# The beginning of a one-core encoder layer: order of the first loads, splits and products changed

## The chip, the cores and the metric

The kernel runs on one core of a Trainium2 chip. The metric is the device time of one launch in microseconds, the median over several runs, lower is better. One further execution is recorded by the hardware profiler; it has a time of its own and a span, which is the time from its first instruction to its last.

## What is computed

One residual layer over 512 tokens of width 1024. All matrix products are of float32 quality.

```python
h = rmsnorm(x, norm_w)                       # x: 512 x 1024
proj = h @ w_in + b_in                       # 11272 columns: q, k, v, gates of two mixers, merge gates
y_m = mlstm(...)                             # 4 heads of 256, chunkwise, conv + SiLU on q and k
y_s = stick_breaking_attention(...)          # 8 heads of 128, rmsnorm on q and k
merged = g_m * (y_m @ w_proj_m) + g_s * (y_s @ w_proj_s)
x = x + merged @ w_out
```

Only the beginning matters here: the rmsnorm of `x`, its transposition, and the first group of 512 columns of `proj` (the first four heads' `q` of the attention).

## The kernel before

**Products in three parts.** Each operand `a` is split into a high part (a rounded copy in the format that TensorE multiplies at full rate) and a low part, `a` minus the high part. A product is three TensorE products: high by high, low by high, high by low. The high part is a copy on ACT or DVE, the low part a subtraction on DVE or POOL.

**Units.** The weights come in units of 512 KB (`Unit`). A unit has a load (`load`, one DMA from the SP queue, line 109), a split (`split`, `wh` on ACT and `wl` on DVE, lines 90 and 91) and products (`mm(0)`, `mm(1)`). The main loop `for c in range(N)` goes through the units in order, splitting some units ahead, and weaves the other work between `mm(0)` and `mm(1)`. All orders are written by hand (the pools run under a manual schedule): an engine executes its instructions in the order in which the program gives them, and an instruction that waits holds up all behind it on that engine.

**The tokens.** `x` lies in four blocks of 128 tokens, `x_t[0]` to `x_t[3]`. `x_scale(tb)` makes the sum of squares of a block on ACT (lines 271 and 274, with a read of the accumulator behind each), the factor on POOL (lines 260 and 261) and multiplies the block on DVE (line 276). `x_turn(tb)` transposes the scaled block on TensorE in two groups of four tiles (line 286) and takes each group out of PSUM as high part `hh` (line 288, one DVE instruction for four tiles) and low part `hl` (line 292, four DVE instructions).

**The first four units are special.** They hold the same 512 columns for eight tiles of the depth, `k` = 0 to 7, two to a unit, and `units[tb]` stands for the products of token block `tb` with all eight (`first_mm(tb)`): 24 products. Their high parts are named `fh` (line 890, ACT), their low parts `fl` (line 891, DVE for the units 0 and 2, POOL for 1 and 3). For each `k` the three products stand side by side: `fh` by `hh` (line 932), `fh` by `hl` (line 933), `fl` by `hh` (line 934).

**What surrounds them.** `warm(n)` issues n products on a tile of zeros (`idle`, line 910). Before the main loop the program gives: nine such products, the transposition of `norm_w` (line 217), `x_scale(0)`, two more, `first_split(0)`, `x_turn(0)`, `first_split(1)` with POOL, `x_scale(1)`, `first_split(2)`, `first_split(3)` with POOL. In the loop, `x_turn(c + 1)` stands between the two halves of units 0 and 1, `x_scale(2)` and `x_scale(3)` stand behind the first of them, and `x_turn(3)` behind the second half of unit 1. The fourth unit's load goes to a tile of another pool (`P5`, shown as `P`).

## Time and profile before

| | |
|---|---|
| median of 3 runs | 719.27 us (718.88 to 719.35) |
| the profiled execution, its own time | 720.13 us |
| its span | 718.4 us |
| TensorE products (PE) busy | 709.8 us, 99% of the span |
| VectorE (DVE) busy | 424.5 us, 59% |
| ScalarE (ACT) busy | 315.8 us, 44% |
| GpSimd (POOL) busy | 93.5 us, 13% |
| mean granted TensorE clock | 0.997 of full |

A step that starts TensorE's dense work earlier or later by a microsecond moves the end by as much, as long as nothing behind it has to wait. All times of instructions are in microseconds from the start of the span.

### The profile page before, as it was taken

What the parts mean: (1) busy time and instruction counts of PE and PEld (TensorE: products, weight loads), DVE (VectorE), ACT (ScalarE), POOL (GpSimd) and SP (SyncE); (2) the same over time, 40 slices, a digit from 0 to 9 for tenths busy, and PEclk for the clock granted to TensorE, in tenths of its full rate; (3) what the DMA queues carried; (4) which work ended last, traced back from release to release, by engine and by line L of the source; (5) the groups of instructions that cost most, each with busy time, mean ns of one, the idle gap of its engine ahead of it and who ended that gap; (6) DMA issues with size and microseconds to landing.
All of it is one profiled execution on the core that took longest, in us unless ns stands there. A gap on an engine that the chain in (4) does not pass through costs nothing.

```text
span 718.4 us, 9058 instructions
## 1 busy us (share of the span) xinstructions
PE 709.8 (99%) x3356; PEld 593.1 (83%) x3356; DVE 424.5 (59%) x663; ACT 315.8 (44%) x601; POOL 93.5 (13%) x235
## 2 busy tenths in 40 slices
PE   7999999999999999999999999999999999999997
PEld 5888888888888888888888888888888888888886
DVE  5837886656487568279944737994343254556441
ACT  5245364476255544244475534447554343222210
POOL 5422022253022112000001110000112000000000
PEclk9999999999999999999999999999999999999999
DMA  6433332233323222333332233333223333333621
GB/s 239 133 103 81 109 86 77 69 95 92 99 62 87 58 86 62 102 91 97 101 94 59 63 99 88 91 100 89 74 59 89 89 91 97 104 88 89 234 89 58
DMA packets 91475, 67.80 MB, mean 94 GB/s; under 512 B 3470, under 2 KB 77608, under 8 KB 91432
## 3 DMA queue, kind: packets, MB, share of 16 engines
q1 hardware_dynamic: 91432, 67.23, 32.8%
q8 instruction: 26, 0.43, 0.2%
q14 instruction: 17, 0.14, 0.1%
HBM read 65.12 MB, written 2.10 MB: 94 GB/s over the span
## 4 chain that ended last, share of the span: by engine, by line
PE 97%; DMA 1%; DVE 1%; POOL 0%; SPq 0%; issue 0%; ACT 0%; DVEq 0%
PE dps L85 28%; PE dps L87 27%; PE dps L86 27%; PE aps L86 2%; PE aps L87 2%; PE aps L85 2%; PE aps L440 1%; PE aps L382 1%; DMA stg<-in_w_in_dram 1%; PE dps L934 1%; PE dps L932 1%; PE dps L933 1%; PE aps L735 1%; PE aps L736 1%; PE aps L737 1%; DVE fl L891 0%
## 5 line engine op out<-in xcount | busy, mean ns | idle before, releaser
L91 DVE TENSOR_TENSOR wl<-stg,wh 128x1024 fp32r<-128x1024 f32 x108 | 132.3, 1225 | 140.3 <-ACT wh L90 139.9
L85 PE MATMUL dps<-hh,wh 128*128 128x512 f32 x448 | 175.8, 392 | 0.0
L86 PE MATMUL dps<-hl,wh 128*128 128x512 f32 x448 | 174.6, 390 | 0.0
L87 PE MATMUL dps<-hh,wl 128*128 128x512 f32 x448 | 174.6, 390 | 0.0
L90 ACT ACTIVATE wh<-stg 128x1024 fp32r<-128x1024 f32 x108 | 113.6, 1052 | 95.3 <-PE dps L87 58.6
L87 PEld LDWEIGHTS dps<-hh,wl 128*128 128x128 f32 x448 | 84.1, 188 | 17.7
L85 PEld LDWEIGHTS dps<-hh,wh 128*128 128x128 f32 x448 | 84.2, 188 | 17.5 <-issue 1.0
L86 PEld LDWEIGHTS dps<-hl,wh 128*128 128x128 f32 x448 | 84.2, 188 | 16.6
L85 PE MATMUL dps<-wh,hh 128*128 128x512 f32 x224 | 88.3, 394 | 0.0
L87 PE MATMUL dps<-wh,hl 128*128 128x512 f32 x224 | 87.4, 390 | 0.0
L86 PE MATMUL dps<-wl,hh 128*128 128x512 f32 x224 | 87.4, 390 | 0.0
L87 PEld LDWEIGHTS dps<-wh,hl 128*128 128x128 f32 x224 | 42.1, 188 | 8.9
L86 PEld LDWEIGHTS dps<-wl,hh 128*128 128x128 f32 x224 | 42.1, 188 | 8.2
L85 PEld LDWEIGHTS dps<-wh,hh 128*128 128x128 f32 x224 | 42.1, 188 | 8.2
L626 DVE SCALAR_TENSOR_TENSOR acc<-tmp,vec,acc 128x511 f32<-128x511 f32 (+2 forms) x48 | 36.0, 750 | 1.7
L629 ACT ACTIVATE tmp<-acc 128x512 f32<-128x512 f32 x16 | 10.1, 633 | 50.2 <-DVE acc L626 50.2
L415 DVE TENSOR_TENSOR_SCAN om<-om 128x512 f32<-128x512 f32 (+3 forms) x32 | 27.9, 871 | 6.3 <-POOL om L409 6.3
L409 POOL TENSOR_SCALAR_AFFINE_SELECT om<-om 128x128 f32<-128x128 f32 x32 | 12.1, 378 | 134.5 <-ACT om L407 134.5
L90 ACT ACTIVATE at_split<-aps 128x384 fp32r<-128x384 f32 (+1 forms) x24 | 11.8, 525 | 36.8 <-PE aps L440 36.8
L688 POOL TENSOR_SCALAR_AFFINE_SELECT w_all<-om 128x128 f32<-128x128 f32 x16 | 4.1, 293 | 168.9 <-DVE om L683 168.9
L91 DVE TENSOR_TENSOR at_split<-aps,at_split 128x384 fp32r<-128x384 f32 (+1 forms) x24 | 13.7, 599 | 19.8 <-ACT at_split L90 19.8
L86 PE MATMUL dps<-wl,mgh 128*128 128x512 f32 x64 | 24.9, 389 | 0.0
(239 smaller groups left out, 1170.6 us busy)
## 6 DMA issues: line engine op xcount, KB each, us to landing
stg<-in_w_in_dram SPq DMA_DIRECT2D x87, 512.0 KB, 3.7
stg<-in_w_proj_s_dram SPq DMA_DIRECT2D x8, 512.0 KB, 3.7
stg<-in_w_proj_m_dram SPq DMA_DIRECT2D x8, 512.0 KB, 3.6
stg<-in_w_out_dram SPq DMA_DIRECT2D x8, 512.0 KB, 3.7
brow<-in_b_in_dram SPq DMA_DIRECT2D x8, 256.0 KB, 4.2
xr<-in_x_dram SPq DMA_DIRECT2D x8, 256.0 KB, 5.7
out_dram<-xr SPq DMA_DIRECT2D x7, 256.0 KB, 2.3
x<-in_x_dram SPq DMA_DIRECT2D x3, 512.0 KB
```

What stands on the lines that cost most here:

```text
L85: nc.tensor.matmul(ps, ah, bh, start=first, stop=False)
L86: nc.tensor.matmul(ps, ah, bl, start=False, stop=False)
L87: nc.tensor.matmul(ps, al, bh, start=False, stop=last)
L90: nc.scalar.activation(hi, src, AF.Copy)
L91: nc.vector.tensor_tensor(lo, src, hi.bitcast(F32), op=OP.subtract)
L382: nc.tensor.transpose(tp[:, tb * 128:(tb + 1) * 128], self.raw[name][tb][:, hs], ident)
L409: nc.gpsimd.affine_select(out=om[:, ts], in_=om[:, ts], compare_op=OP.is_gt, fill=1.0, base=0, channel_multiplier=1, pattern=[[-1, 128]])
L415: nc.vector.tensor_tensor_scan(back, back, back, 1.0, op0=OP.mult, op1=OP.bypass)
L440: nc.tensor.transpose(tp[:, at + (i - j) * 128:at + (i - j + 1) * 128], a_t[i][:, j * 128:(j + 1) * 128], ident)
L626: nc.vector.scalar_tensor_tensor(acc[:, j:], t[:, 0:T - j], cw(3 - j, ch), acc[:, j:], op0=OP.mult, op1=OP.add)
L629: nc.scalar.activation(t, acc, AF.Sigmoid)
L735: nc.tensor.matmul(nm[:, 0:258], ph, vh, start=j == 0, stop=False)
```

## The change

The loads are issued as x block 0, units 0, 1, 2, x block 1, unit 3, x blocks 2 and 3 (before: x block 0, `norm_w`, units 0 and 1, x block 1, units 2 and 3, x blocks 2 and 3). `norm_w` is loaded from the ACT queue. `x_scale` is cut in two functions: `x_square` (ACT) and `x_scale` (POOL and DVE), for block 0 with the multiplication in two halves and one POOL instruction fewer. `x_turn` takes only three of the eight groups' `hh` on DVE; the others go to ACT, in four copies each (line 299 of the new program), and the `hl` come later, as functions that are called behind both groups. The first splits are cut into `first_high` (ACT, line 903) and `first_low` (line 908): the first four low parts go to POOL, the last four to DVE behind `x_scale(1)`. The products of a token block are put in another order: `first_a` gives `fh` by `hh` and `fh` by `hl` (line 955), `first_b` gives `fl` by `hh` (line 959). For block 0 all of them stand ahead of `x_turn(1)`.

```diff
--- before.py
+++ after.py
@@ -104,9 +104,9 @@
             self.slow = None
             self.heavy = False
 
-        def load(self, tag="stg"):
+        def load(self, tag="stg", by=None):
             self.st = blk(tag, shape=self.shape)
-            nc.sync.dma_start(self.st, self.ap)
+            (by or nc.sync).dma_start(self.st, self.ap)
 
         def split(self):
             self.wh = blk("wh", FR, self.shape)
@@ -200,7 +200,7 @@
     def rows(dst, lo, src, n):
         nc.sync.dma_start(dst[lo:lo + n, :], src.rearrange("(r p) -> r p", p=128))
 
-    rows(v_rows, 0, norm_w, 8)
+    nc.scalar.dma_start(v_rows[0:8, :], norm_w.rearrange("(r p) -> r p", p=128))
     ident = cst.tile([128, 128], F32, name="ident")
     make_identity(nc, ident)
     mhalf = cst.tile([128, 8], F32, name="mhalf")
@@ -260,37 +260,51 @@
         nc.gpsimd.tensor_scalar(dst, ssq, 1.0 / n, eps, op0=OP.mult, op1=OP.add)
         nc.gpsimd.tensor_tensor(dst, dst, mhalf[:, 0:dst.shape[1]], op=OP.pow)
 
-    def x_scale(tb):
+    def x_square(tb):
         xs = tiny.tile([128, 4], F32, name="xs", bufs=2)
-        ssq, r = xs[:, 0:2], xs[:, 2:3]
         xn = x_t[tb]
         junk = blk("om", BF, (D,), name="junk")
-        if tb == 0:
-            for i in range(2):
-                c = slice(i * D // 2, (i + 1) * D // 2)
-                nc.scalar.activation(junk[:, c], xn[:, c], AF.Square, accum_out=ssq[:, i:i + 1])
-            nc.gpsimd.tensor_tensor(ssq[:, 0:1], ssq[:, 0:1], ssq[:, 1:2], op=OP.add)
-        else:
-            nc.scalar.activation(junk, xn, AF.Square, accum_out=ssq[:, 0:1])
-        rstd(r, ssq[:, 0:1], D, EPS)
-        nc.vector.tensor_scalar(xn, xn, r, None, op0=OP.mult)
+        n = 2 if tb == 0 else 1
+        for i in range(n):
+            c = slice(i * D // n, (i + 1) * D // n)
+            nc.scalar.activation(junk[:, c], xn[:, c], AF.Square, scale=D ** -0.5, accum_out=xs[:, i:i + 1])
+        return xs
+
+    def x_scale(tb, xs):
+        xn = x_t[tb]
+        r = xs[:, 2:3]
+        n = 2 if tb == 0 else 1
+        nc.gpsimd.tensor_scalar(r, xs[:, 0:1], xs[:, 1:2] if tb == 0 else 0.0, EPS, op0=OP.add, op1=OP.add)
+        nc.gpsimd.tensor_tensor(r, r, mhalf[:, 0:1], op=OP.pow)
+        for i in range(n):
+            c = slice(i * D // n, (i + 1) * D // n)
+            nc.vector.tensor_scalar(xn[:, c], xn[:, c], r, None, op0=OP.mult)
 
     def x_turn(tb):
         ts = slice(tb * 128, (tb + 1) * 128)
         xn = x_t[tb]
+        low = []
         for g in range(2):
             ks = slice(4 * g, 4 * g + 4)
             tp = att_ps()
             for j in range(4):
                 kt = g * 4 + j
                 nc.tensor.transpose(tp[:, j * 128:(j + 1) * 128], xn[:, kt * 128:(kt + 1) * 128], ident)
-            dh = hh[:, ks, ts]
-            nc.vector.tensor_tensor(dh, tp.rearrange("p (k t) -> p k t", k=4),
-                                    nw_t[:, ks].unsqueeze(2).to_broadcast([128, 4, 128]), op=OP.mult)
-            for j in range(4):
-                k = 4 * g + j
-                nc.vector.scalar_tensor_tensor(hl[:, k, ts], tp[:, j * 128:(j + 1) * 128], nw_t[:, k:k + 1],
-                                               hh[:, k, ts].bitcast(F32), op0=OP.mult, op1=OP.subtract)
+            if tb == 0 or tb == 1 and g == 0:
+                nc.vector.tensor_tensor(hh[:, ks, ts], tp.rearrange("p (k t) -> p k t", k=4),
+                                        nw_t[:, ks].unsqueeze(2).to_broadcast([128, 4, 128]), op=OP.mult)
+            else:
+                for j in range(4):
+                    k = 4 * g + j
+                    nc.scalar.activation(hh[:, k, ts], tp[:, j * 128:(j + 1) * 128], AF.Copy, scale=nw_t[:, k:k + 1])
+
+            def lows(g=g, tp=tp):
+                for j in range(4):
+                    k = 4 * g + j
+                    nc.vector.scalar_tensor_tensor(hl[:, k, ts], tp[:, j * 128:(j + 1) * 128], nw_t[:, k:k + 1],
+                                                   hh[:, k, ts].bitcast(F32), op0=OP.mult, op1=OP.subtract)
+            low.append(lows)
+        return low
 
     def bias_row(c0):
         b = blk("brow")
@@ -883,18 +897,20 @@
 
     f_w = []
 
-    def first_split(i, low=None):
-        u = units[i]
+    def first_high(i):
         for j in range(2):
             hi, lo = blk("qk", FR, name="fh"), blk("y", FR, name="fl")
-            nc.scalar.activation(hi, u.st[:, j, :], AF.Copy)
-            (low or nc.vector).tensor_tensor(lo, u.st[:, j, :], hi.bitcast(F32), op=OP.subtract)
+            nc.scalar.activation(hi, units[i].st[:, j, :], AF.Copy)
             f_w.append((hi, lo))
+
+    def first_low(k, eng=None):
+        hi, lo = f_w[k]
+        (eng or nc.vector).tensor_tensor(lo, units[k // 2].st[:, k % 2, :], hi.bitcast(F32), op=OP.subtract)
 
     units[0].load()
     units[1].load()
+    units[2].load()
     load_x(1)
-    units[2].load()
     units[3].load("P5")
     load_x(2)
     load_x(3)
@@ -911,27 +927,52 @@
 
     warm(9)
     norm_vec()
-    x_scale(0)
+    xs0 = x_square(0)
+    warm(3)
+    x_scale(0, xs0)
+    first_high(0)
+    first_high(1)
+    low0 = x_turn(0)
     warm(2)
-    first_split(0)
-    x_turn(0)
-    first_split(1, nc.gpsimd)
-    x_scale(1)
-    first_split(2)
-    first_split(3, nc.gpsimd)
-
-    f_ps = []
+    low0[0]()
+    low0[1]()
+    for k in range(4):
+        first_low(k, nc.gpsimd)
+    first_high(2)
+    xs1 = x_square(1)
+    first_high(3)
+    x_scale(1, xs1)
+    for k in range(4, 8):
+        first_low(k)
+
+    f_ps = [None] * TB
+
+    def first_a(tb, ks):
+        if 0 in ks:
+            f_ps[tb] = dense_ps()
+        for p in range(2):
+            for k in ks:
+                nc.tensor.matmul(f_ps[tb], h_sta(k, tb)[p], f_w[k][0], start=p == 0 and k == 0, stop=False)
+
+    def first_b(tb, ks):
+        for k in ks:
+            nc.tensor.matmul(f_ps[tb], h_sta(k, tb)[0], f_w[k][1], start=False, stop=k == KT - 1)
+
+    lo_k, hi_k = range(4), range(4, 8)
 
     def first_mm(tb):
         def mm(half):
-            if half == 0:
-                f_ps.append(dense_ps())
-            for k in range(4 * half, 4 * half + 4):
-                sh, sl = h_sta(k, tb)
-                wh, wl = f_w[k]
-                nc.tensor.matmul(f_ps[tb], sh, wh, start=k == 0, stop=False)
-                nc.tensor.matmul(f_ps[tb], sl, wh, start=False, stop=False)
-                nc.tensor.matmul(f_ps[tb], sh, wl, start=False, stop=k == KT - 1)
+            if tb == 0 and half == 0:
+                first_a(0, range(0, 2))
+                first_a(0, range(2, 4))
+                first_a(0, range(4, 6))
+                first_b(0, range(0, 4))
+                first_a(0, range(6, 8))
+                first_b(0, range(4, 8))
+            elif tb:
+                ks = hi_k if half else lo_k
+                first_a(tb, ks)
+                first_b(tb, ks)
         return mm
 
     for tb in range(TB):
@@ -992,10 +1033,12 @@
         ahead(c)
         units[c].mm(0)
         if c < 2:
-            x_turn(c + 1)
+            low = x_turn(c + 1)
+            low[0]()
+            low[1]()
         if c == 0:
-            x_scale(2)
-            x_scale(3)
+            for tb in (2, 3):
+                x_scale(tb, x_square(tb))
             gates_fill()
         for g in list(act):
             if c in REST:
@@ -1010,7 +1053,8 @@
                 act.append(g)
         units[c].mm(1)
         if c == 1:
-            x_turn(3)
+            for fn in x_turn(3):
+                fn()
     now[0] = N
     units[N - 1].evac()
     assert not act and not pend and not later, (act, pend, later)
```

On POOL, at the beginning: `xs` are the factors of the token blocks (the instruction that writes from `xs` and `mhalf` is the last step of a factor), `fl` the low parts of the first weights. Before, from the factor of block 0 on:

```order
L261 TENSOR_TENSOR xs<-xs,mhalf 128x1
L891 TENSOR_TENSOR fl<-stg,fh 128x512 x2
L260 TENSOR_SCALAR xs<-xs 128x1
L261 TENSOR_TENSOR xs<-xs,mhalf 128x1
L891 TENSOR_TENSOR fl<-P_114,fh 128x512 x2
L260 TENSOR_SCALAR xs<-xs 128x1
```

and with the change:

```order
L278 TENSOR_TENSOR xs<-xs,mhalf 128x1
L908 TENSOR_TENSOR fl<-stg,fh 128x512 x4
L277 TENSOR_SCALAR xs<-xs 128x1
L278 TENSOR_TENSOR xs<-xs,mhalf 128x1
L277 TENSOR_SCALAR xs<-xs 128x1
```

All four low parts that POOL makes now stand ahead of the factor of block 1; before, two stood ahead of it and two behind.

On DVE, at the same place: `x` are the token blocks that are multiplied by their factors. Before, from the multiplication of block 0 on:

```order
L276 TENSOR_SCALAR x<-x,xs 128x1024
L891 TENSOR_TENSOR fl<-stg,fh 128x512 x2
L288 TENSOR_TENSOR hh<-aps,nw_t 128x4x128
L292 SCALAR_TENSOR_TENSOR hl<-aps,nw_t,hh 128x128 x4
L288 TENSOR_TENSOR hh<-aps,nw_t 128x4x128
L292 SCALAR_TENSOR_TENSOR hl<-aps,nw_t,hh 128x128 x4
L276 TENSOR_SCALAR x<-x,xs 128x1024
L891 TENSOR_TENSOR fl<-stg,fh 128x512 x2
L288 TENSOR_TENSOR hh<-aps,nw_t 128x4x128
```

and with the change:

```order
L281 TENSOR_SCALAR x<-x,xs 128x512 x2
L294 TENSOR_TENSOR hh<-aps,nw_t 128x4x128 x2
L304 SCALAR_TENSOR_TENSOR hl<-aps,nw_t,hh 128x128 x8
L281 TENSOR_SCALAR x<-x,xs 128x1024
L908 TENSOR_TENSOR fl<-stg,fh 128x512 x2
L908 TENSOR_TENSOR fl<-P_114,fh 128x512 x2
L294 TENSOR_TENSOR hh<-aps,nw_t 128x4x128
L304 SCALAR_TENSOR_TENSOR hl<-aps,nw_t,hh 128x128 x8
L281 TENSOR_SCALAR x<-x,xs 128x1024 x2
```

DVE makes no low part of a weight ahead of `hh` and `hl` of block 0 now, and four of them, not two, behind the multiplication of block 1.

On ACT, from the squares of block 0 on (`junk` takes the squares, `xs` their sum; `fh` are the high parts of the first weights). Before:

```order
L271 ACTIVATE junk,xs<-x 128x512 x2
L890 ACTIVATE fh<-stg 128x512 x4
L274 ACTIVATE junk,xs<-x 128x1024
L890 ACTIVATE fh<-stg 128x512 x2
L890 ACTIVATE fh<-P_114 128x512 x2
L274 ACTIVATE junk,xs<-x 128x1024 x2
L337 ACTIVATE sqj,ssq<-qraw 128x128 x4
```

and with the change:

```order
L270 ACTIVATE junk,xs<-x 128x512 x2
L903 ACTIVATE fh<-stg 128x512 x6
L270 ACTIVATE junk,xs<-x 128x1024
L903 ACTIVATE fh<-P_114 128x512 x2
L299 ACTIVATE hh<-aps,nw_t 128x128 x4
L270 ACTIVATE junk,xs<-x 128x1024 x2
L351 ACTIVATE sqj,ssq<-qraw 128x128 x4
L299 ACTIVATE hh<-aps,nw_t 128x128 x16
```

The squares of blocks 2 and 3 (the row with `x2` at the end) stood right behind the last `fh`; now the four copies of `hh` that need the transposed block 1 stand ahead of them.

## Rows read from the trace of the kernel before

**Rows 1.** The page: busy time and share of the span, instructions.

```profile
PE 709.8 (99%) x3356; PEld 593.1 (83%) x3356; DVE 424.5 (59%) x663; ACT 315.8 (44%) x601; POOL 93.5 (13%) x235
```

**Rows 2.** Waits of TensorE: engine, line, awaited, us in total, times, longest.

```profile
PE dps L934 <- DVE fl L891: 0.4, 1, 0.4
```

**Rows 3.** Timeline of TensorE, 10 to 27 us: start, duration, instruction, count, idle before.

```profile
10.66 0.64 PE L932 MATMUL dps<-fh,hh 128*128 128x512 f32 x1 [2.43 <-DVE hh L288]
...
15.09 1.03 PE L286 MATMUL aps<-ident,x 128*128 128x128 f32 x8
15.88 0.48 PE L932 MATMUL dps<-fh,hh 128*128 128x512 f32 x1
...
17.68 0.50 PE L934 MATMUL dps<-fl,hh 128*128 128x512 f32 x1 [0.41 <-DVE fl L891]
...
19.40 0.39 PE L932 MATMUL dps<-fh,hh 128*128 128x512 f32 x1
...
22.13 1.03 PE L286 MATMUL aps<-ident,x 128*128 128x128 f32 x8
...
26.53 0.48 PE L932 MATMUL dps<-fh,hh 128*128 128x512 f32 x1
```

**Rows 4.** Stretches: us, busy and count by engine, clock, DMA share, GB/s.

```profile
3.00:3.50 0.50, 0.50 (x3) 0.40 (x2) 0.00 (x0) 0.01 (x1) 0.00 (x0) 1.00 0.88 334
3.50:4.50 1.00, 1.00 (x4) 0.81 (x3) 0.00 (x0) 1.00 (x3) 0.00 (x0) 1.00 0.78 124
4.50:13.00 8.50, 6.07 (x20) 3.96 (x20) 5.23 (x13) 4.94 (x10) 3.77 (x7) 0.87 1.03 397
8.23:10.66 2.43, 0.00 (x1) 0.03 (x1) 2.01 (x4) 2.16 (x5) 0.66 (x1) 1.00 1.05 410
10.66:14.11 3.45, 3.45 (x8) 2.64 (x9) 3.38 (x10) 3.23 (x6) 2.96 (x5) 0.52 0.98 343
```

**Rows 5.** Timeline of the SP queue, its issues from 1.6 to 3.1 us.

```profile
1.68 0.36 SPq L201 DMA_DIRECT2D v_rows<-in_norm_w_dram  x1
2.08 0.90 SPq L109 DMA_DIRECT2D stg<-in_w_in_dram  x2
```

**Rows 6.** Timeline of ACT, 7 to 17 us.

```profile
7.96 1.15 ACT L890 ACTIVATE fh<-stg 128x512 fp32r<-128x512 f32 x2 [3.12 <-DMA stg<-in_w_in_dram]
9.29 1.15 ACT L890 ACTIVATE fh<-stg 128x512 fp32r<-128x512 f32 x2 [0.19 <-DMA stg<-in_w_in_dram]
...
14.44 1.06 ACT L274 ACTIVATE junk<-x 128x1024 bf16<-128x1024 f32 x1 [0.24 <-DMA x<-in_x_dram]
15.41 0.19 ACT L274 ACTIVATION_READ_ACCUMULATOR junk<-x 128x1 f32 x1
```

**Rows 7.** Timeline of POOL, 9.9 to 17.1 us.

```profile
10.00 2.51 POOL L891 TENSOR_TENSOR fl<-stg,fh 128x512 fp32r<-128x512 f32 x2 [3.96 <-ACT fh L890]
12.60 0.19 POOL L260 TENSOR_SCALAR xs<-xs 128x1 f32<-128x1 f32 x1
...
13.76 3.32 POOL L891 TENSOR_TENSOR fl<-P,fh 128x512 fp32r<-128x512 f32 x2 [0.33 <-ACT fh L890]
```

**Rows 8.** Timeline of DVE, 8 to 17.6 us.

```profile
8.62 1.29 DVE L891 TENSOR_TENSOR fl<-stg,fh 128x512 fp32r<-128x512 f32 x2 [1.72 <-ACT fh L890]
9.83 0.68 DVE L288 TENSOR_TENSOR hh<-aps,nw_t 128x512 fp32r<-128x512 f32 x1
10.55 1.13 DVE L292 SCALAR_TENSOR_TENSOR hl<-aps,nw_t,hh 128x128 fp32r<-128x128 f32 x4
...
13.47 0.75 DVE L276 TENSOR_SCALAR x<-x,xs 128x1024 f32<-128x1024 f32 x1
14.14 3.49 DVE L891 TENSOR_TENSOR fl<-stg,fh 128x512 fp32r<-128x512 f32 x2
```

**Rows 9.** ACT, 107.2 to 109 us: 128x128 copies out of PSUM.

```profile
107.32 0.37 ACT L407 ACTIVATE om<-aps,rq 128x128 f32<-128x128 f32 x1
107.57 0.38 ACT L411 ACTIVATE a_all<-aps,rq 128x128 f32<-128x128 f32 x1
```

## Prediction

> **What bounds the kernel now.** The page comes first: TensorE is busy for 709.8 of 718.4 us [rows 1], so time is to be had only where TensorE waits or runs at half clock. The waits say where that is: the last thing it waits for is a low part `fl`, once, 0.4 us [rows 2]. The timeline puts that wait at 17.68 us [rows 3]; from there to the end the product stream has no other wait. So the end follows one number, the moment at which TensorE has done a given amount of work. I take the first product of block 2 (before: 26.53 us, behind 48 products and the transpositions of all four blocks) as the mark. In the changed program the same work stands ahead of that product, so the difference at the mark is the difference at the end, unless something later is starved.
>
> Ahead of 17.68 us three things cost: a wait of 2.43 us for `hh` [rows 3]; then eight products in 3.45 us at a mean granted clock of 0.52 (the lower of the two levels, 1.2 GHz), where about 15 would have fit at 0.227 us each [rows 3, 4]; then the wait for `fl`. That wait comes from a chain on POOL and DVE: two `fl` on POOL take 2.51 us from 10.00, then the factor of block 1 follows and its multiplication on DVE at 13.47, then two `fl` on DVE take 3.49 us, since two on POOL run beside them and take 3.32 [rows 7, 8]. Alone, two on DVE took 1.29 us [rows 8].
>
> **The change, part by part.** I count from L, the landing of unit 0. Before, L is about 7.95: ACT's first `fh` starts at 7.96, released by the DMA [rows 6].
>
> Loads. Without `norm_w` on SP's queue the issue of unit 0 moves from 2.08 to 1.68 [rows 5]. What the landing gains is not in the trace. Below: nothing. Above: 0.40 of issue, and in the second after 3.50 the engines moved 124 GB/s where they later moved 397 [rows 4], so 0.69 us more if that dip went with it; 1.1 together. In 3.00 to 3.50 they still carried 334 GB/s of x [rows 4], so an earlier issue mostly queues behind x; I take half the issue, 0.20. L = 7.75.
>
> By the Trainium skill ("DMA: Bandwidth & Descriptors", section "Issuing engines are not separate DMA queues"), a DMA from another engine runs on the same 16 DMA engines and saves only the issuing time; no run here shows that. It would bar the 0.69; with the whole 0.40, L would be 7.55 and the sum below 0.20 smaller.
>
> The other loads follow at (14.44 - 7.96) / 5 = 1.30 us each [rows 6]. Block 1 of x goes behind unit 2, so it lands at L + 3.9; its square (0.97 to the read, 0.19 for the read [rows 6]) is over at about L + 5.1, hidden, since POOL is not yet ready for it. The third warm product, the halved multiplication and the POOL instruction saved for block 0 all end ahead of its `hh`, near 8.5, which the chain below does not wait for; I cost them at nothing, and at most at the 0.4 of a product were the chain shorter.
>
> The POOL chain. From ACT's start on an `fh` to POOL's start on its `fl` is 10.00 - 9.29 = 0.71 [rows 6, 7]: L + 0.72. Four `fl` by 2.51 a pair: 5.02, to L + 5.74. They run while DVE takes `hh` and `hl` out of PSUM, as the pair of before did (9.83 to 13.4 [rows 8]), so I keep its price. From the end of the pair (12.51) to the multiplication on DVE (13.47) is 0.96 [rows 7, 8]: L + 6.70. DVE's next starts 0.67 later (14.14 - 13.47). Four `fl`, undisturbed now: starts 1.21 / 2 = 0.605 apart, the last 0.69 long, 2.50 in all [rows 8]. The last is ready at L + 9.87, and its product starts 0.05 later, L + 9.92 = 17.67. Before, the stalled product started at 17.68 [rows 3]. The chain is as long as the one it replaces: it drops the contention (3.49 against 1.29 a pair) and puts two more POOL `fl` and two more DVE `fl` into the line.
>
> TensorE up to there. Its other 23 products for block 0 fit in between: `hh` comes some 2 us earlier because no `fl` stands ahead of it on DVE, and the clock need not be lower. That is a real gain in work done early, but the last product waits for the chain. The 2.43 us wait and the half clock (about 1.6 us) are gone from one place and come back as waits for `fl`.
>
> Block 1. Before, it was transposed at 15.09, inside the products of block 0, so its `hh` was ready long before 19.40 [rows 3]. Now the transposition stands behind all 24: it starts 0.23 after 17.67, at 17.90. Eight take 1.03 with the next product 0.79 after the start, 0.10 apart, so four are out after 1.03 - 0.40 = 0.63: 18.53. Then `hh` on DVE 0.68, and 0.15 to the product as at 10.66 [rows 3, 8]: 19.36, against 19.40 before. Up to here nothing is won or lost.
>
> Block 2, the new wait. Between the halves of block 1 stands the transposition of block 2, and it needs `x_scale(2)`. Its square ran on ACT at 14.44, as soon as it landed [rows 6]. Now four copies of `hh` stand ahead of it on ACT, which wait for block 1's second transposition: 17.90 + 1.03 = 18.93. The trace has no such copy; the nearest are 128x128 out of PSUM, 0.25 apart and 0.38 long [rows 9]; bounds are nothing and the 0.68 that DVE takes for the whole group [rows 8] put in place of the 1.0. The square starts at 19.95 and is read out at 19.95 + 1.16 = 21.11; POOL 0.08 later, from there to DVE 0.87 (12.60 to 13.47 [rows 7, 8]): 22.06; the multiplication 0.75, TensorE 0.06 later: 22.87. TensorE gets there at 19.36 + 2.73 = 22.09 (twelve products, 19.40 to 22.13 [rows 3]). So it waits 0.78. Queued behind the copies on ACT are both squares, and for these wait POOL's factors, DVE's multiplications and both transpositions.
>
> Then 0.79 + 2.73 + 0.79 to the mark: 27.18 against 26.53, **0.65 us later**. Block 3's factor follows block 2's by about 1.25 and is needed 3.5 later: hidden. `hh` of blocks 2 and 3 on ACT come behind the four squares of the first result, I make it just in time; if not, the cost is tenths. The split of unit 4 moves behind them, and the products of blocks 2 and 3 (48 at 0.227) cover it.
>
> The sum against the profiled execution is 720.13 + 0.65 = 720.78; the median lies 0.86 below it, so 719.27 + 0.65 = **719.9 us**. That is inside 0.2% (1.4 us), about what a measurement of this kernel tells from no change.
>
> **The rivals.**
>
> *The clock falls (slower).* From about 14.8 us, when the first 20 products are done, to 19.4 TensorE has only four products, 0.6 us apart, and one transposition. Before, the granted clock went to the lower level after the 2.43 us without any product [rows 3, 4]. For it: the stretch is longer, 4.6 us. Against it: no gap in it is longer than about 1.1 us. Price: eight products in 3.45 us instead of 1.82 [rows 4], 1.6 us; the wait of 0.78 covers part of it, so 0.9 to 1.6 net; twice that stretch, up to 2.5. Together 720.8 to 722.4, 721.5 in the middle. It decides once the clock stays low for about 2.5 us past 19.4.
>
> *Earlier landings, faster POOL.* L is 6.85, and POOL's `fl` are quicker where DVE is idle. The first gives 0.90. The second is bounded by block 1's square: L + 5.1, then 0.08 and 0.87, gives the multiplication at L + 6.0 in place of L + 6.70, so at most 0.7. Time 719.9 - 0.9 - 0.7 = 718.3. For it: the dip of 124 GB/s. Against the second: POOL's 1.26 was measured beside DVE reading PSUM, and only DVE's `fl` stretched it, to 1.66 [rows 7, 8].
>
> The Trainium skill ("SBUF — State Buffer", section "SBUF: two separate sides") has VectorE operations with two SBUF inputs and GpSimd exclude each other for whole instructions. The stretching of both agrees (3.49 against 1.29 on DVE); by it the 1.26 is POOL's own pace, and this rival keeps only its 0.9.
>
> *The change delivers what its order suggests (clearly faster).* All 24 products of block 0 would run at full rate as their operands land, with no wait behind. Block 0 would then be over near 14.9 and not 17.9, 3 us early: 716.9. Against it stand the four `fl` on POOL and the factor of block 1 behind them; it needs POOL's chain to be half as long as its rows say.
>
> **How the numbers follow.** No change worth the name, by the sum: 0.65 (its own range 718.6 to 720.6, from L 1.1 earlier up to L not earlier, and half a microsecond of late copies). The clock: 0.20. Earlier landings: 0.10. Clearly faster: 0.05. Of the sum's cases all are within 0.2%; of the clock's most are slower by more; of the earlier landings a third is faster by more. That gives faster 0.09, same 0.71, slower 0.20. The range is 718.3 to 721.9.
>
> **What the profile will show.** Four `fl` back to back on POOL, some 5 us, from about 8.5; the multiplication of block 1 on DVE at 14.4; four `fl` on DVE in 2.5 us; the last product of block 0 at 17.7; ACT idle from 14.1 to 18.9 and then the copies ahead of the square of block 2; a wait of TensorE of 0.8 us before the transposition of block 2; the first product of block 2 at 27.2. I am wrong if POOL's four take much less than 5 us, if the first landing moves by a microsecond, if the clock drops near 18 us, or if something behind 40 us waits for a unit's split.

## The result: 3.56 us slower

The changed kernel takes 722.64 us (median of 4 runs, 722.42 to 722.80); the kernel before 719.08 (718.66 to 719.35). The ratio is 1.0049, 95% interval 1.0037 to 1.0062: slower by 3.56 us, 0.5%. Forecast were 719.9 us and a range of 718.3 to 721.9, so the time lies above it. The traces of the two profiled executions show 2.7 of the 3.56 us, since the execution behind the rows above took 720.13 us, 1 us more than the other executions of that kernel. Why is part of the answer.

### The profile page after: what moved, and what is told of

Read it like the earlier page. It is cut to its first block, busy times and chain, and to the rows that moved or that the text cites. A ratio compares the mean times of both kernels' runs of the same rounds, so it can differ in the third digit from the quotient of the medians.

```text
span 721.1 us, 9076 instructions
## 1 busy us (share of the span) xinstructions
PE 712.2 (99%) x3359; PEld 591.9 (82%) x3359; DVE 419.6 (58%) x659; ACT 321.1 (45%) x621; POOL 92.3 (13%) x234
## 4 chain that ended last, share of the span: by engine, by line
PE 96%; DMA 1%; SPq 1%; DVE 1%; ACT 1%; POOL 0%; issue 0%; DVEq 0%
PE dps L85 27%; PE dps L86 27%; PE dps L87 27%; PE aps L86 2%; PE aps L87 2%; PE aps L85 2%; PE aps L454 1%; PE dps L955 1%; PE aps L396 1%; DMA stg<-in_w_in_dram 1%; SPq L201 1%; PE aps L749 1%; PE aps L750 1%; PE aps L751 1%; PE dps L959 1%; PE aps L776 0%
## 5 line engine op out<-in xcount | busy, mean ns | idle before, releaser
L85 PE MATMUL dps<-yh,wh 128*128 128x512 f32 x64 | 24.9, 389 | 0.0
```

Source lines behind the costliest of these rows:

```text
L85: nc.tensor.matmul(ps, ah, bh, start=first, stop=False)
```

## The profile after

Busy time from the page of the changed kernel (span 721.1 us):

```profile
PE 712.2 (99%) x3359; PEld 591.9 (82%) x3359; DVE 419.6 (58%) x659; ACT 321.1 (45%) x621; POOL 92.3 (13%) x234
```

The stretches that answer to [rows 4] (us, busy and count by engine, clock, DMA share, GB/s):

```profile
10.00:12.00 2.00, 1.98 (x7) 0.86 (x5) 1.30 (x6) 1.85 (x4) 2.00 (x3) 1.00 1.05 418
12.00:14.00 2.00, 1.65 (x6) 1.05 (x6) 0.00 (x0) 1.84 (x4) 1.96 (x2) 1.00 1.03 378
14.00:16.00 2.00, 1.47 (x5) 0.78 (x5) 1.03 (x2) 0.46 (x1) 0.81 (x2) 1.00 0.39 80
16.00:18.00 2.00, 1.42 (x3) 0.56 (x3) 2.00 (x4) 0.00 (x0) 0.00 (x0) 1.00 0.04 7
```

TensorE's granted clock is 1.00 in all of them, where [rows 4] has 0.52 from 10.66 to 14.11, and the products agree: the pair at 9.75 in the timeline below takes 0.47 us to the next start, 0.235 each, against 0.43 each there. The half clock is gone, and the rival of a falling clock did not come. TensorE's waits (what waited for what, us in total, times, longest):

```profile
PE dps L959 <- DVE fl L908: 0.9, 1, 0.9
PE aps L292 <- DVE x L281: 0.7, 1, 0.7
PE dps L955 <- ACT hh L299: 0.5, 1, 0.5
PE dps L955 <- DVE hh L294: 0.3, 1, 0.3
PE dps L959 <- POOL fl L908: 0.3, 1, 0.3
```

Where [rows 2] had one wait behind the first product there are five. The timeline of TensorE answers to [rows 3]: transposition of block 1 at 18.52, first product of block 1 at 19.90, transposition of block 2 at 23.57, first product of block 2, the mark, at 28.79 (before 26.53), first product of unit 4 at 40.69.

```profile
8.89 1.02 PE L955 MATMUL dps<-fh,hh 128*128 128x512 f32 x2
9.75 0.63 PE L955 MATMUL dps<-fh,hl 128*128 128x512 f32 x2
10.22 1.02 PE L955 MATMUL dps<-fh,hh 128*128 128x512 f32 x2
...
16.37 2.31 PE L959 MATMUL dps<-fl,hh 128*128 128x512 f32 x4 [0.89 <-DVE fl L908]
18.52 1.03 PE L292 MATMUL aps<-ident,x 128*128 128x128 f32 x8
19.90 1.19 PE L955 MATMUL dps<-fh,hh 128*128 128x512 f32 x4 [0.34 <-DVE hh L294]
...
23.57 1.09 PE L292 MATMUL aps<-ident,x 128*128 128x128 f32 x8 [0.65 <-DVE x L281]
...
28.79 1.27 PE L955 MATMUL dps<-fh,hh 128*128 128x512 f32 x4 [0.47 <-ACT hh L299]
29.95 1.27 PE L955 MATMUL dps<-fh,hl 128*128 128x512 f32 x4
31.07 1.09 PE L959 MATMUL dps<-fl,hh 128*128 128x512 f32 x4
...
40.69 0.39 PE L85 MATMUL dps<-wh,hh 128*128 128x512 f32 x1
```

The timeline of ACT, which answers to [rows 6]: unit 0 lands at 8.21, later than before and not earlier; the copies of `hh` of blocks 2 and 3 come at 28.39, last in line behind the squares of the first result (the first of them at 26.78).

```profile
8.21 1.15 ACT L903 ACTIVATE fh<-stg 128x512 fp32r<-128x512 f32 x2 [2.60 <-DMA stg<-in_w_in_dram]
...
19.59 1.14 ACT L299 ACTIVATE hh<-aps,nw_t 128x128 fp32r<-128x128 f32 x4 [5.13 <-PE aps L292]
20.61 1.07 ACT L270 ACTIVATE junk<-x 128x1024 bf16<-128x1024 f32 x1
...
26.78 0.31 ACT L351 ACTIVATE sqj<-qraw 128x128 bf16<-128x128 f32 x1 [3.97 <-DVE qraw L342]
...
28.39 4.22 ACT L299 ACTIVATE hh<-aps,nw_t 128x128 fp32r<-128x128 f32 x16
```

DVE, from the multiplication of block 1 on: that of block 2 takes 0.75 us as that of block 1 does, that of block 3, the same instruction, 1.87, and the first result (`qraw`) leaves PSUM behind it.

```profile
14.97 0.75 DVE L281 TENSOR_SCALAR x<-x,xs 128x1024 f32<-128x1024 f32 x1 [3.67 <-POOL xs L278]
...
22.76 0.75 DVE L281 TENSOR_SCALAR x<-x,xs 128x1024 f32<-128x1024 f32 x1 [0.72 <-POOL xs L278]
24.28 1.87 DVE L281 TENSOR_SCALAR x<-x,xs 128x1024 f32<-128x1024 f32 x1 [0.77 <-POOL xs L278]
26.07 0.67 DVE L342 TENSOR_TENSOR qraw<-dps,brow 128x512 f32<-128x512 f32 x1
```

And POOL, which answers to [rows 7]: the four `fl` take 5.04 us, though DVE stands idle from 11.30 on (14.97 - 3.67), so the rival of a POOL that is faster beside an idle DVE did not come; and beside the long multiplication run the first two memsets of `gates_fill`.

```profile
8.92 5.04 POOL L908 TENSOR_TENSOR fl<-stg,fh 128x512 fp32r<-128x512 f32 x4 [2.25 <-ACT fh L903]
...
24.19 0.95 POOL L496 MEMSET wg<- 128x1024 f32 x1
25.09 0.52 POOL L499 MEMSET sel<- 36x512 f32 x1
```

## The experiments

L is the landing of unit 0, taken as the start of ACT's first `fh` (by this reading the 7.95 of the prediction is 7.96); the mark is the first product of block 2. "Chain" is mark minus L. Differences are medians against the kernel before in the same set of runs (the changed kernel: +3.56).

**One wait at a time.** Four kernels, each the changed kernel with one edit.

Squares of blocks 2 and 3 early, off the place behind the copies of `hh`:

```diff
     first_high(3)
+    xs23 = [x_square(2), x_square(3)]
     x_scale(1, xs1)
...
-                x_scale(tb, x_square(tb))
+                x_scale(tb, xs23[tb - 2])
```

> The changed kernel with one edit: the squares of blocks 2 and 3 stand on ACT right behind the last high part of the first weights, ahead of the copies of hh of block 1. Theory A (what is lost is lost behind ACT's order: the squares wait for the transposition of block 1, and with them the multiplications, the first result's squares and the copies of hh of block 2): the wait of 0.65 us ahead of the transposition of block 2 and the waits of block 2's products (0.47, and 0.4 more in their spacing) go, first product of block 2 at about 27.1 instead of 28.79, time about 720.5 (2.1 us less than 722.6). Rival B (the loss comes from the landing of the first weights and the chain of low parts on POOL, and the later waits only show it): the waits move, and the time stays within 0.4 us of 722.6.

Measured: 721.07 (720.37 to 721.87), +2.26. Its mark:

```profile
27.16 1.17 PE L956 MATMUL dps<-fh,hh 128*128 128x512 f32 x4
```

With L at 8.10 the chain is 19.1, where the changed kernel has 20.6. Both waits of blocks 1 and 2 (0.7 and 0.5) are gone. In the trace all is as expected. The time is half a microsecond above what I gave it; in four of the five executions the mean clock is 0.996 to 0.998, where the changed kernel has 0.998 to 0.999. Whether that is the reason is open: the profiled execution, at 1.000, took 720.77.

`hh` of every block on DVE again:

```diff
-            if tb == 0 or tb == 1 and g == 0:
+            if True:
```

> The changed kernel with one edit: all hh come out of PSUM on DVE, none on ACT. Theory A: the squares of blocks 2 and 3 run as soon as x lands, but DVE now has both groups of block 1 ahead of the multiplication of block 2, so the wait ahead of the transposition of block 2 stays at about 0.65; the wait of block 2's products for ACT (0.47 and 0.4) goes: first product of block 2 near 27.8, time about 721.3. Rival B (landing and POOL chain): within 0.4 us of 722.6. Rival C (DVE has too much to do without ACT's help): slower than 722.6.

Measured: 720.85 (720.35 to 721.44), +2.04. L 7.67, mark 27.18, chain 19.5; of the wait at the transposition of block 2, 0.28 is left, and the wait for `hh` of block 2 is gone. I had expected the mark 0.6 later: the squares start at 14.11, before anything waits for them.

`gates_fill` one block later, so that its memsets don't run beside DVE's multiplications:

```diff
+        if c == 1:
             gates_fill()
```

> The changed kernel with one edit: POOL's four memsets and two selects for the gates stand one unit later, so they do not run beside DVE's multiplication of block 3, which took 1.87 us beside them and 0.75 alone. Theory A: that multiplication takes 0.75 at 24.3, the first result is evacuated at 25.0 and not at 26.1, ACT reaches the copies of hh of block 2 about 1.0 earlier, before TensorE needs them: the wait of 0.47 and the 0.4 behind it go, first product of block 2 at 28.1, time about 721.5 (1.1 less). Rival (ACT would be late all the same, or POOL's fill is not what stretched the multiplication): multiplication still above 1.5 us, time 722.6.

Measured: 721.43 (720.94 to 722.61), +2.62. The timeline of DVE in this kernel:

```profile
24.04 0.75 DVE L281 TENSOR_SCALAR x<-x,xs 128x1024 f32<-128x1024 f32 x1 [0.76 <-POOL xs L278]
24.70 0.68 DVE L342 TENSOR_TENSOR qraw<-dps,brow 128x512 f32<-128x512 f32 x1
```

The multiplication of block 3 takes 0.75 again, `hh` of blocks 2 and 3 starts at 27.04, the wait for it is gone; the one at the transposition of block 2 stays (0.65). L 7.96, mark 27.80, chain 19.84.

Two of POOL's four `fl` to DVE:

```diff
-        first_low(k, nc.gpsimd)
+        first_low(k, nc.gpsimd if k < 2 else None)
```

> The changed kernel with one edit: the low parts of k = 2 and 3 go to DVE, behind hl of block 0, where DVE was idle for 3.67 us; POOL keeps k = 0 and 1. Theory A (the chain of four low parts on POOL, then the factor of block 1, sets the end of block 0's products): POOL is free at 11.4, the factor of block 1 starts when its square has been read (13.2) and not at 14.04, the multiplication of block 1 at 14.1 instead of 14.97, everything behind it 0.85 earlier, time about 721.8. Rival (something else, the landing of unit 3 or of x, holds block 0's products): last product of block 0 still at 18.2, time 722.6.

Measured: 721.71 (721.63 to 722.19), +2.90. First product of block 1 at L + 11.1 where the changed kernel has L + 11.7. Each edit alone is thus worth 0.7 to 1.5 us; the first two remove the same waits.

**Loads and order.** The kernel before, with nothing but the change's loads (`norm_w` on ACT's queue, unit 2 ahead of block 1 of x):

> The kernel before with the change's loads alone: norm_w on ScalarE's queue, unit 2 ahead of block 1 of x. Theory: the landing of unit 0 does not come earlier for it (7.6 to 8.2 us, as in all five kernels with these loads), while block 1 of x lands some 1.3 us later, its square on ScalarE (10.53 before) starts near 11.9, the squares' factor on GpSimd and the four low parts behind it (13.76 on GpSimd, 14.14 on VectorE) slip by about as much, and the last products of block 0 by 0.5 to 1.1. Time 719.5 (719.0 to 720.2). Rival, the loads in the changed order pay: unit 0 lands by 7.5 and the time is 718.4 or below.

Measured: 719.79 (719.39 to 720.80) against 718.99, ratio 1.0014 (1.0004 to 1.0023). L 8.04. The loads alone cost 0.8 us. My reason, the later block 1 of x, could not yet be told from the landing of unit 0. TensorE at its beginning:

```profile
10.74 0.76 PE L932 MATMUL dps<-fh,hh 128*128 128x512 f32 x1 [1.58 <-DVE hh L288]
11.31 0.63 PE L933 MATMUL dps<-fh,hl 128*128 128x512 f32 x1
11.73 0.63 PE L934 MATMUL dps<-fl,hh 128*128 128x512 f32 x1
12.16 0.63 PE L932 MATMUL dps<-fh,hh 128*128 128x512 f32 x1
```

The products come 0.43 apart, as at the half clock of [rows 4], yet the clock of this profile is 1.00 in every stretch from 8 to 20 us: its record can miss a fall, and the products' spacing has to be read beside it.

The changed kernel with the transposition of block 1 between the halves of block 0 again:

```diff
+                first_b(0, range(0, 4))
+            elif tb == 0:
                 first_a(0, range(4, 6))
-                first_b(0, range(0, 4))
                 first_a(0, range(6, 8))
                 first_b(0, range(4, 8))
-            elif tb:
+            else:
```

> The changed kernel with the transposition of block 1 put back between the halves of block 0's products (4 weight rows ahead of it, 4 behind). Theory: what the changed order loses is that the transposition of block 1 stands behind all of block 0, though its input is ready 6.8 us behind the landing and the last low parts only 9.2 us behind it. With it in the middle, hh of block 1 is copied while block 0's second half runs, ScalarE's squares of blocks 2 and 3 start near 17.1 instead of 20.6, the wait of 0.65 at the transposition of block 2 goes, first product of block 1 near 19.2, first product of block 2 near 26.6, time 720.4 (719.9 to 721.0). Rival, the four low parts on GpSimd set the end of block 0 anyway: first product of block 1 at 19.9 as in the changed kernel, time 722 or more.

Measured: 720.86, +1.87, but ten executions spread from 718.34 to 722.74. The profiled one (719.69) has the first product of block 1 at 18.85, the mark at 25.99, a chain of 18.4: the order is worth 2.2 us of the chain. For the spread, a second profile of this kernel:

> The kernel with the transposition of block 1 between the halves of block 0, whose ten executions spread over 718.3 to 722.7 us where the other kernels spread over 0.5 to 1.5. Theory: TensorE's waits of 0.64, 0.73 and 1.27 us between 11.8 and 15.2 let the granted clock fall in some executions; if this one is above 721.5 a stretch of clock 0.5 to 0.6 stands between 11 and 20 us and the first product of block 2 is at 27.5 to 28.5; if it is below 720 the clock is 1 throughout and that product is at 25.5 to 26.2. Rival: the spread is that of the landings, which then differ from 7.6 by 2 us or more, at a clock of 1.

It took 720.95, between my two cases, with the same L (7.61 against 7.63). Two stretches of the first execution (us, busy by engine, then clock, DMA share, GB/s):

```profile
14.00:15.00 1.00, 0.00 (x0) 0.00 (x0) 0.64 (x1) 0.00 (x0) 0.33 (x1) 1.00 0.35 85
15.00:16.00 1.00, 0.83 (x8) 0.83 (x9) 1.00 (x3) 0.00 (x0) 0.00 (x0) 1.00 0.08 12
```

and the same of the second:

```profile
14.00:15.00 1.00, 0.00 (x0) 0.00 (x0) 0.66 (x1) 0.35 (x1) 0.31 (x1) 0.77 0.82 214
15.00:16.00 1.00, 0.85 (x4) 0.85 (x5) 1.00 (x3) 0.00 (x0) 0.00 (x0) 0.50 0.38 53
```

After the same idle time of TensorE (1.27 and 1.26 us, behind shorter waits of 0.64 and 0.73 in the first and 0.29 and 0.73 in the second) the clock stayed at 2.4 GHz in the one and went to 1.2 GHz until nearly 18 us in the other. The ten timed executions order themselves by it: mean clock 0.999 to 1.000 for 718.34, 719.24 and 719.69, 0.997 for 720.45 to 721.44, 0.995 for 722.70 to 722.74. So the rival of a falling clock is real for this order, and most of the spread goes with the clock; the 1.35 us between 718.34 and 719.69, both at 0.999, do not.

Squares early, `gates_fill` later and two `fl` on DVE, all three:

> The changed kernel with three edits tried one by one: squares of blocks 2 and 3 called early, gates_fill one block later, low parts 2 and 3 on VectorE. By the single traces the first product of block 1 comes 11.1 us behind the landing (as with the low parts moved alone) and that of block 2 7.4 us later (as with the squares early): 18.5 us behind the landing, where the changed kernel has 20.6. Theory, the waits are in series and the gains add to that: time 720.4 (719.8 to 720.9), all waits of TensorE in blocks 1 and 2 under 0.4. Rival, the edits remove the same wait: no better than the best of them alone, 720.9 to 721.2.

Measured: 719.87 (719.60 to 720.17), +0.88. L 7.73, first product of block 1 at L + 10.9, mark at L + 18.3. That is 2.7 us below the changed kernel, where the three alone gave 1.3, 0.9 and 0.7: the waits are in series and the gains add.

**Second profiles.** The kernel before:

> The kernel before, unchanged, for a second profiled execution: the first lay 1.1 us above the median of its other executions, so that 0.9 of the 3.6 us between the two kernels stand in no trace. Theory: the missing time lies ahead of the first product of block 2 (26.53 in the first profile), in the landing of unit 0 or in the half clock between 10.66 and 14.11, so that a profiled execution of 718.9 to 719.2 has it at 25.3 to 25.7. Rival: it lies later in the program, and the first product of block 2 is at 26.4 to 26.6 again.

Measured: 719.16, and the missing time is at the beginning, as the theory had it. From its timelines of ACT, TensorE and POOL:

```profile
6.31 1.15 ACT L890 ACTIVATE fh<-stg 128x512 fp32r<-128x512 f32 x2 [1.51 <-DMA stg<-in_w_in_dram]
8.32 1.15 ACT L890 ACTIVATE fh<-stg 128x512 fp32r<-128x512 f32 x2 [0.86 <-DMA stg<-in_w_in_dram]
```

```profile
9.02 0.47 PE L932 MATMUL dps<-fh,hh 128*128 128x512 f32 x1 [1.08 <-ACT fh L890]
...
13.34 1.09 PE L286 MATMUL aps<-ident,x 128*128 128x128 f32 x8 [1.20 <-DVE x L276]
...
16.71 0.50 PE L934 MATMUL dps<-fl,hh 128*128 128x512 f32 x1 [0.72 <-DVE fl L891]
...
25.56 0.48 PE L932 MATMUL dps<-fh,hh 128*128 128x512 f32 x1
```

```profile
9.03 2.55 POOL L891 TENSOR_TENSOR fl<-stg,fh 128x512 fp32r<-128x512 f32 x2 [3.03 <-ACT fh L890]
```

and the stretch that had a clock of 0.52 in [rows 4]:

```profile
10.66:14.11 3.45, 2.25 (x14) 1.63 (x13) 2.71 (x6) 3.02 (x6) 2.91 (x4) 1.00 0.98 342
```

Unit 0 lands at 6.31 and not 7.96, unit 1 at 8.32 and not 9.29, so `fl` and then `hh` are ready earlier on DVE, TensorE starts at 9.02 and not 10.66, and the clock stays up. Most of that does not reach the mark: TensorE now waits 1.20 us for the multiplication of block 1 and 0.72 for `fl`. What reaches the mark is 0.97 us, and POOL's first `fl`, that of unit 1, starts earlier by the same 0.97 (9.03 against 10.00 [rows 7]); the mark comes 16.53 behind it in both profiles. By this equality the kernel before hangs in these two executions on unit 1 through POOL's chain, and the 2.43 us wait and the half clock of [rows 3, 4] cost it nothing in the end. Of 64 timed executions of this kernel in the three larger sets three are above 720 us: the execution behind [rows 1 to 9] was an unusual one.

The changed kernel:

> The changed kernel, unchanged, for a second profiled execution. Theory: the chain behind the landing is the same to 0.2 us (first product of block 1 at 11.7 behind the landing of unit 0, first product of block 2 at 20.6, waits at the transposition of block 2 and at ScalarE's copies of block 2), and the profiled time differs from 722.8 by the difference of the landing (8.20 in the first) alone. Rival: the waits move among the engines from execution to execution, and the first product of block 2 lies more than 0.5 us off that.

Measured: 722.30. L 7.71, first product of block 1 at 19.40, mark at 28.29: chain 20.58 in both, the same waits to 0.1 us.

**Which of the loads.** Four kernels. The changed kernel with `norm_w` on SP's queue again:

```diff
-    nc.scalar.dma_start(v_rows[0:8, :], norm_w.rearrange("(r p) -> r p", p=128))
+    rows(v_rows, 0, norm_w, 8)
```

> The changed kernel with norm_w loaded through SyncE again; unit 2 stays ahead of block 1 of x. Theory N (the 16 small packets of norm_w, on ScalarE's queue beside SyncE's, make some of the 16 DMA engines late): unit 0 lands near 6.3 to 6.9 as in the second profile of the kernel before (6.31), and the chain behind it, 20.6 long, moves with it: time 721.3 (720.8 to 721.8). Theory U (three units ahead of block 1 of x spread the same engines' time over more transfers): unit 0 lands at 7.6 to 8.2 as in all eleven profiles with the changed loads, time 722.6. Theory E (executions differ by chance): anything between, with an 0.5 us spread.

Measured: 721.21 (720.87 to 722.24) against 719.12, +2.09. From the timelines of ACT and TensorE:

```profile
6.88 1.15 ACT L903 ACTIVATE fh<-stg 128x512 fp32r<-128x512 f32 x2 [1.34 <-DMA stg<-in_w_in_dram]
```

```profile
27.46 1.27 PE L955 MATMUL dps<-fh,hh 128*128 128x512 f32 x4 [0.47 <-ACT hh L299]
```

The chain is 20.58 again and moved with the landing: the landing is 1.33 earlier than in the first profile of the changed kernel, the time 1.32 less (721.48 against 722.80). The changed kernel with unit 2 behind block 1 of x, `norm_w` on ACT's queue:

```diff
-    units[2].load()
     load_x(1)
+    units[2].load()
```

> The changed kernel with unit 2 behind block 1 of x again; norm_w stays on ScalarE's queue. Theory N (norm_w's queue): unit 0 lands at 7.6 to 8.2, block 1 of x is there 1.3 us earlier but its factor waits behind GpSimd's four low parts, so the time is 722.4 (722.0 to 722.9). Theory U (three units in a row): unit 0 lands near 6.3 to 6.9 and the time is 721.3.

Measured: 722.63 (722.50 to 722.77), +3.51; L 7.58. This half of the edit costs nothing in the time. The kernel before with `norm_w` alone moved:

> The kernel before with nothing but norm_w moved to ScalarE's queue. Theory N: unit 0 lands at 7.6 to 8.2 in place of the 6.31 of the second profile of before, its hh waits behind the low parts of unit 0 on VectorE, TensorE waits over 2 us at the first product as in the first profile of before (2.43) and the granted clock may fall behind that: time 719.8 (719.4 to 720.4), as with all of the loads moved (719.79). Theory U: no change, 718.9.

Measured: 719.95 (719.06 to 720.96), ratio 1.0011 (1.0002 to 1.0020). L 7.95, a wait of 2.38 us ahead of the first product, the clock at 0.50 from 10 to 16 us in the profiled execution. All as theory N has it, and as much as all the loads cost together. In this execution TensorE waits for no `fl`: POOL starts at 9.95, but the half clock lasts so long that the mark, at 27.03, comes 17.08 behind it and not 16.53.

**All repairs.** The changed kernel with two `fl` on POOL and six on DVE, the transposition of block 1 ahead of block 0's last four products, `hh` of block 1 on ACT, the square of block 2 early, `gates_fill` later and the bias row loaded ahead of the small vectors:

```diff
-            if tb == 0 or tb == 1 and g == 0:
+            if tb == 0:
...
+    for fn in later.pop(0, []):
+        fn()
     load_vecs()
...
-        first_low(k, nc.gpsimd)
+        first_low(k, nc.gpsimd if k < 2 else None)
...
+    xs2 = x_square(2)
+    for k in range(4, 6):
+        first_low(k)
     x_scale(1, xs1)
-    for k in range(4, 8):
+    for k in range(6, 8):
...
-                first_b(0, range(4, 8))
...
             low = x_turn(c + 1)
+            if c == 0:
+                first_b(0, range(4, 8))
...
-                x_scale(tb, x_square(tb))
+                x_scale(tb, x_square(tb) if tb == 3 else xs2)
+        if c == 1:
             gates_fill()
```

> The changed kernel with every place mended that the traces show to wait: low parts 2 to 5 on VectorE, 4 and 5 ahead of block 1's scaling; the transposition of block 1 ahead of the last four low products of block 0; hh of block 1 on ScalarE alone; square of block 2 behind unit 3's copies; gates_fill one block later; the bias row loaded ahead of the small vectors. First product of block 1 expected 9.5 us behind the landing (changed kernel 11.7, before 11.45), that of block 2 16.9 (20.6, 18.6). Theory, the beginning is a chain of these waits: time 718.6 (717.8 to 719.5), at or a little below the kernel before. Rival, VectorE with six of eight low parts is now the bound: block 1 not earlier than 11 us behind the landing, time 720 or more.

Measured: 718.07 (717.88 to 718.42, 11 runs) against 718.99 (33 runs): ratio 0.9987, interval 0.9978 to 0.9996: 0.9 us faster than the kernel before and 4.5 us below the changed one. TensorE in this kernel:

```profile
15.06 1.09 PE L292 MATMUL aps<-ident,x 128*128 128x128 f32 x8 [0.16 <-DVE x L281]
15.91 1.17 PE L964 MATMUL dps<-fl,hh 128*128 128x512 f32 x4
16.92 1.08 PE L960 MATMUL dps<-fh,hh 128*128 128x512 f32 x4
...
24.32 1.17 PE L960 MATMUL dps<-fh,hh 128*128 128x512 f32 x4
```

Block 1 starts at L + 9.3, the mark is at L + 16.7; one wait of 0.16 us is left behind the first product. The same with `norm_w` on SP's queue:

> The kernel with all repairs (718.07), with norm_w loaded through SyncE again. Theory N: unit 0 lands near 6.3 to 6.9 where it landed at 7.64, the last of the four units and block 1 of x some 0.6 earlier, and since block 1's factor and the last low parts hang on those two, about 0.6 of it reaches the end: time 717.4 (717.0 to 717.8). Theory U: no change, 718.1.

Measured: 718.13 (717.75 to 718.31). The expected 0.6 us did not come; its profiled execution had L at 7.82, late in spite of the queue, and the mark at L + 16.7 as without the edit. The price that theory N gives came in the changed kernel and in the kernel before, not in this one; whether the landing stays late here or something else bounds the beginning was not tried.

## Why the prediction was wrong

In both profiles of before, the time is 693.60 us more than the mark (720.13 - 26.53, 719.16 - 25.56); in both of the changed kernel 694.01 (722.80 - 28.79, 722.30 - 28.29). So the medians put the mark at 25.48 before and at 28.63 after: 3.15 us, and 0.41 behind it. Forecast for the median was 27.18 - 0.86 = 26.32. (One slip in the sum's own range changes nothing here: a landing 1.1 before 7.95 is 0.9 before the sum's 7.75, and gives 719.0, not 718.6.) The miss, 2.31 us at the mark and 0.41 behind it, has three parts.

**Landing, 1.2 us.** "What the landing gains is not in the trace. Below: nothing": the bound did not reach below nothing, and that step failed; its sign of being wrong, a first landing that moves by a microsecond, came, but to the late side. With `norm_w` on ACT's queue unit 0 landed at 7.58 to 8.21 in all 13 profiles; on SP's queue at 6.31, 6.88, 7.82 and 7.96 in four. The order of the bulk loads has no part in it (+3.51 against +3.56). In times, 1.43 of the 3.56 us go with the queue of `norm_w` (722.64 against 721.21), and 2.09 are left with it on SP's.

The second half of this step was to take the profiled execution's offset to the median, 0.86, as one that carries over. It does not. The offset is that of an execution of before in which unit 1, and with it POOL's chain, was 0.97 late; the changed kernel's chain begins with unit 0, and that lands late in both its profiles (8.21 and 7.71). With the offset taken off, the forecast's 26.32 and its chain of 19.43 stand for a landing at 6.89; the median of the changed kernel, 28.63 with a chain of 20.58, for one at 8.05. (Both are worked out, not measured.) In the same way the five times with `norm_w` on SP's queue stand for landings from 6.28 to 7.65, the four of the changed kernel for 7.83 to 8.21, an estimate from the constant 20.58 and 694.01.

Shown is that the moved load costs this time in these two kernels, and in the changed kernel that it does so through the landing. Not shown is why. The edit does two things at once: it puts sixteen small packets on a second queue, and it lets unit 0 be issued at 1.68 and not 2.08. Which of the two makes it late was not tried. The Trainium skill ("DMA: Bandwidth & Descriptors", section "Issuing engines are not separate DMA queues") says that all queues share the 16 DMA engines and another issuing engine saves only issue time. It bars a gain, rightly; the loss of 0.8 us (kernel before) to 1.4 us (changed kernel) it doesn't give.

**From the landing to the mark, 1.15 us.** Forecast 27.18 - 7.75 = 19.43, measured 20.58. Most steps held. POOL's four took 5.04 (5.02), block 1's multiplication came at L + 6.76 (L + 6.70), the first product of block 1 at L + 11.69 (L + 11.61), the wait at the transposition of block 2 was 0.65 (0.78), that transposition at L + 15.36 (L + 15.12): 0.24 late in sum. The step that failed is the next: "`hh` of blocks 2 and 3 on ACT come behind the four squares of the first result, I make it just in time; if not, the cost is tenths", beside "Block 3's factor ... hidden". From that transposition to the mark it is 5.22 us, not 4.31: 0.9 us. The factor of block 3 was hidden from TensorE, but the multiplication that uses it stands ahead of `qraw` on DVE; it took 1.87 us beside POOL's memsets, `qraw` went at 26.07, ACT's four squares at 26.78, the copies at 28.39, the product at 28.79. With the memsets elsewhere the same multiplication took 0.75, this wait was gone, and the mark came at L + 19.84, 0.74 earlier. I had not followed what stands behind that instruction, nor what POOL does beside it. The Trainium skill ("SBUF — State Buffer", section "SBUF: two separate sides") has a VectorE operation in a two-port mode and a GpSimd operation exclude each other from the shared ports for a whole instruction. The trace goes the same way, 1.87 against 0.75 with memsets of 0.95 and 0.52 beside it, but the 1.12 more is the length of neither, and that the multiplication is in such a mode no run shows.

**Behind the mark, 0.4 us.** "unless something later is starved" was my condition, and it failed in small: block 2's first eight products go at the pace of ACT's copies (4.22 for 16, the 0.25 apart of [rows 9]), 1.16 and 1.12 us for four (28.79, 29.95, 31.07) where four at full rate take 0.91. With the squares early, where these copies are ahead of the products, the time is 693.61 more than the mark (720.77 - 27.16), and with that back at the 693.60 of the kernel before.

Right were the balance of the two chains up to block 1 (the half clock and the 2.43 us come back as waits for `fl`; the second profile of before shows the same trade inside one kernel), the wait for the squares, and the clock, which stayed full. That rival had its chance in the order: with another place for one transposition the clock fell.

## What to carry to other kernels

Before a profile becomes the base of a sum, compare its time with the median of the other executions; if it differs by more than the effect that is looked for, find out where, for the offset need not carry over to the changed kernel. Where work is moved behind an engine's queue, follow that queue to its next consumer and ask for each instruction what runs beside it on the other engines. Waits in a beginning are in series: each repair alone gave 0.7 to 1.5 us of the 3.6, and all together were 0.9 us faster than the kernel before.

## What was not expected of the hardware

A load of 16 small packets, moved from the queue of the bulk loads to another engine's queue, goes with a later first bulk load, though that one is issued 0.40 us earlier: 7.58 to 8.21 us in 13 profiles against 6.31 to 7.96 in four, and 0.8 us in the time of the kernel before. A DVE multiplication of 128x1024 took 1.87 us beside two POOL memsets, which have no input, and 0.75 without them. After nearly the same idle time of TensorE (1.27 and 1.26 us) the granted clock stayed at its upper level in one execution of a kernel and fell in another. And in one profile (the loads alone) the granted clock was recorded as 1.00 where the products came at half rate, 0.43 us apart.
